# Two transformer blocks on one core: block exchange issued by SyncE, second and third blocks of x by halves

## The chip, the cores and the metric

One Trainium2 chip, one of its cores. The metric is device time in microseconds (us) of one launch that runs both blocks; before the change it is 2243.42 us, the median of three runs (2242.3 to 2247.32). A time is a run of the whole program; a profile is one more execution, with its own time.

## The reference

256 tokens of width 2048 pass through two transformer blocks in float32. The first has a softmax attention with forget gates and a feed-forward part with a causal convolution; the second mixes four gated-linear-attention heads and eight dilated-attention heads, and has a gated feed-forward part.

```python
# first block
a = rms_norm(x, mix_norm)
q, k, v, f = split(a @ fox_w_in)             # 16 heads of 128
q, k = rms_norm(q, q_gain), rms_norm(k, k_gain)
cum = cumsum(log_sigmoid(f + b_f))
p = softmax(causal(q @ k.T * scale + cum_q - cum_k))
h = x + (p @ v) @ fox_w_out
up = rms_norm(h, ffn_norm) @ ffn_w_up        # 2 x 5632 wide
y = conv_b + sum(conv_w[t] * shifted(up, 2 - t) for t in range(3))
gate, val = split(y)
h = h + (silu(gate) * val) @ ffn_w_down
# second block
proj = rms_norm(h, norm1_g) @ w_in_2         # gla q, k, v, r, gate; dilated q, k, v
mix = concat(gla(...) * silu(r), dilated(rms_norm(qb), rms_norm(kb), vb))
h = h + mix @ w_out_2
h2 = rms_norm(h, norm2_g)
out = h + (silu(h2 @ w_gate) * (h2 @ w_up)) @ w_down
```

## The kernel before, in words

Every large product is done by `gemm`. A weight block of 512 rows by 512 columns (1 MB of float32) is loaded into a `raw` tile (`dma_to`, L154; three buffers), split in two halves of a K step each into a rounded part `wh` (ScalarE, ACT, L105) and a rest `wl` (VectorE, DVE, L111), and multiplied as three products, `wh` by the high part of the activations, `wl` by the high part, `wh` by the low part (TensorE, PE, L118 to L120). One unit is such a half: 12 matmuls of 512 columns. `split_to` works four units ahead of the matmuls, with five `wh`/`wl` buffers. The raw buffers come free when the `wl` of their second half is done, so the load of a block waits for DVE.

After each unit `pump` advances the generators in flight by one `yield`: evacuations of finished products (`fast`) and attention (`slow`). So the code's order of emission, unit by unit, sets each engine's order, and each engine and each queue works strictly in that order.

The products leave PSUM with tokens on the partitions; most must be turned so that features are. `flip` (L308) does it without TensorE: DVE transposes 32 by 32 blocks into `turn` (L312), a unit later `exchange` sends `turn` to a DRAM buffer `way` in four DMAs of 128 KB (L303), a unit after that one DMA of 512 KB brings it back with blocks in place (L318), and four units later ACT reads it (`ordered`, L328). Attention's `turned` does the same with the softmax weights (L480, L303, L489). In the kernel before, L303, L318 and L489 are issued by GpSimd's queue (POOL), among POOL's own arithmetic (normalising q and k, L241, L242, L392; the bias tiles `pb`), the loads of forget-gate sums `ckb` (L647, four DMAs of 512 KB that wait for `cum_dram`, L643), and the residual stream's `h` and `home` (L260, L264). SyncE's queue (SP) issues the weights.

`resid` adds the product to `h` (L347). For the first three column blocks it flips `h`; for the last one TensorE transposes it (`transposes`, L290). The `sc` matmuls (L442, L443) read flipped q and k.

At the start `x` comes transposed in four blocks of 512 rows, `xr`; `prep_x` splits a block's four 128-row tiles into high and low (ACT L107, DVE L113). The first block comes by ACT's queue in quarters, the second, third and fourth by SP's (L274), each ahead of its weight block, whose load is in two halves for blocks 1 and 2 (L152). `split_to` prepares a whole block of `x` before the first half of its weight block.

Of the kernel before, what the change touches and what calls it, by code (L numbers as in the profile page):

```python
# [21 lines left out]
KG = D // 512  # L22
# [21 lines left out]
def fox_gla_dilated_kernel(  # L44
# [20 lines left out]
    nc = tc.nc  # L65
# [15 lines left out]
    def alloc(shape, dt, name):  # L81
        i = free_slots.popleft()
        t = slots.tile([P] + shape, dt, tag=f"s{i}", name=name)
        slot_of[id(t)] = (i, t)
        return t

    def free(*ts):
        for t in ts:
            i, _ = slot_of.pop(id(t))
            free_slots.append(i)  # L90
# [9 lines left out]
    def col(c, n=1):  # L100
        return cols[:, c:c + n]

    def hi_of(out_, in_, scale=None):
        if scale is None:
            act.copy(out_, in_)  # L105
        else:
            act.activation(out=out_, in_=in_, func=AF.Copy, scale=scale)  # L107

    def lo_of(out_, in_, hi, scale=None):
        if scale is None:  # L110
            dve.tensor_tensor(out=out_, in0=in_, in1=hi.bitcast(F32), op=ALU.subtract)  # L111
        else:
            dve.scalar_tensor_tensor(  # L113
                out=out_, in0=in_, scalar=scale, in1=hi.bitcast(F32), op0=ALU.mult, op1=ALU.subtract
            )
# [11 lines left out]
    def prep_x(kg, kts=range(4)):  # L127
        for kt in kts:
            d = x_tiles[kg * 2 + kt // 2][:, kt % 2]
            g_ = col(C_MIX + kg * 4 + kt)  # L130
            hi_of(d[:, 0], xr[kg][:, kt], g_)
            lo_of(d[:, 1], xr[kg][:, kt], d[:, 0], g_)
            if kt == 3:
                free(xr[kg])
# [4 lines left out]
    def dma_to(i):  # L139
        while next_dma[0] <= min(i, len(plan) - 1):  # L140
            k = next_dma[0]
            t = rawp.tile([P, 4, 512], F32, tag="raw", name="raw")
            src = plan[k].rearrange("p (k c) -> p k c", c=512)
            if k == 0:
                for q in range(4):
                    nc.sync.dma_start(out=t[:, q], in_=src[:, q])
            else:
                if k < KG:
                    load_x(k)
                if k < 3:  # L150
                    for q in (slice(0, 2), slice(2, 4)):
                        nc.sync.dma_start(out=t[:, q], in_=src[:, q])  # L152
                else:
                    nc.sync.dma_start(out=t, in_=src)  # L154
                if k == 3:
                    nc.sync.dma_start(out=cols[:, C_FFN:], in_=cols_d[:, C_FFN:])
                    nc.sync.dma_start(out=wn, in_=w_n.rearrange("p (a k c) -> p a k c", a=2, c=16))
                if k == 8:
                    nc.sync.dma_start(out=const, in_=const_d)
                if 4 <= k < 8:  # L160
                    fetch(k - 4, nc.sync)
            raw_t[k] = t
            next_dma[0] += 1

    def split_to(u, mid=None):
        while next_spl[0] <= min(u, 2 * len(plan) - 1):
            k = next_spl[0]
            dma_to(k // 2 + NRAW - 1)
            if k in (2, 4, 6):
                prep_x(k // 2)  # L170
            r = raw_t[k // 2][:, (k % 2) * 2:(k % 2) * 2 + 2]
            wh = splp.tile([P, 2, 512], F32R, tag="wh", name="wh")
            wl = splp.tile([P, 2, 512], F32R, tag="wl", name="wl")
            if k < 2:
                for q in range(2):
                    if mid:
                        mid(2 * k + q)
                    hi_of(wh[:, q], r[:, q])
                    lo_of(wl[:, q], r[:, q], wh[:, q])
            else:  # L180
                hi_of(wh, r)
                lo_of(wl, r, wh)
            spl_t[k] = (wh, wl)
            if k % 2:
                raw_t.pop(k // 2)
            next_spl[0] += 1
# [26 lines left out]
    def gemm(xt, kgs, evac, ready=None, last=False):  # L213
        acc = [accp.tile([P, 512], F32, tag="a", name=f"acc{t}") for t in range(2)]
        n = 0
        tot = 4 * len(kgs)
        for kg in kgs:
            while ready is not None and not ready(kg):
                pump()
            for half in range(2):  # L220
                u = unit[0]
                unit[0] += 1
                split_to(u + LEAD)
                wh, wl = spl_t.pop(u)
                xx = xt[kg * 2 + half]
                pairs = [(t, kk) for t in range(2) for kk in range(2)]
                for t, kk in sorted(pairs, key=lambda p: p[1]) if u < 2 else pairs:
                    sl = slice(t * P, (t + 1) * P)
                    mm3(acc[t], xx[:, kk, 0, sl], xx[:, kk, 1, sl], wh[:, kk], wl[:, kk],
                        n + kk == 0, n + kk == tot - 1)  # L230
                n += 2
                if last:
                    free(xx)
                if n == tot:
                    start_fast(evac(acc))
                else:
                    pump()
# [20 lines left out]
    def fetch(c, queue=nc.gpsimd):  # L258
        h[c] = alloc([2, 512], F32, f"h{c}")
        queue.dma_start(out=h[c], in_=home[c])  # L260
# [6 lines left out]
    xr = [alloc([4, S], F32, f"xr{i}") for i in range(KG)]  # L267
    wn = cpool.tile([P, 2, 16, 16], F32, name="wn")
    gqk = cpool.tile([P, 2], F32, name="gqk")

    def load_x(i, kt=None):
        src = x_t[i].rearrange("p (k c) -> p k c", c=S)
        if kt is None:
            nc.sync.dma_start(out=xr[i], in_=src)  # L274
        else:
            nc.scalar.dma_start(out=xr[i][:, kt], in_=src[:, kt])

    rows = {}

# [20 lines left out]
    def exchange(turn, width):  # L300
        way = ways.tile([P, 4, S], F32, tag="way", name="way")
        for i in range(4):
            nc.gpsimd.dma_start(out=way[:, i, 0:width].rearrange("(j c) e -> c j e", c=32),  # L303
                              in_=turn[32 * i:32 * i + 32, :, 0:width])
        return way[:, :, 0:width]

    def flip(src, into=None):
        turn = alloc([4, S], F32, "turn")  # L308
        sv = src.rearrange("p t (k q c) -> p t q k c", q=4, c=32)
        qv = turn.rearrange("p q (k t r) -> p t q k r", t=2, r=32)  # L310
        for t in range(2):
            dve.transpose(out=qv[:, t], in_=sv[:, t])  # L312
        yield
        way = exchange(turn, S)
        yield
        held = alloc([4, S], F32, "flip") if into is None else into
        f = held.rearrange("p a c -> p (a c)").rearrange("p (i e) -> p i e", i=4)
        nc.gpsimd.dma_start(out=f, in_=way)  # L318
        for _ in range(4):
            yield  # L320
        return f.rearrange("p i (k t r) -> p k t i r", k=4, t=2), held, turn
# [93 lines left out]
    def attention(box, gqk, bias_of, ot, done, tag, flipped, ready=None):  # L415
# [58 lines left out]
        def turned(pairs):  # L474
            held = {}
            for a in pairs:
                turn = alloc([4, S], F32, "pturn")
                for n in range(2):
                    pb = sm.pop(a + n)
                    dve.transpose(  # L480
                        out=turn[:, :, n * 96:(n + 1) * 96].rearrange("p j (c r) -> p j c r", c=3),
                        in_=pb[:, 0].rearrange("p (c j r) -> p j c r", c=3, j=4),
                    )
                    free(pb)
                yield
                way = exchange(turn, 192)
                yield
                held[a] = turn
                nc.gpsimd.dma_start(out=turn[:, :, 0:192], in_=way)  # L489
            for _ in range(3):  # L490
                yield
            for a in pairs:
                f = held[a][:, :, 0:192].rearrange("p i (n c r) -> p n c i r", n=2, c=3)
                for n in range(2):
                    pt[a + n] = alloc([3, P], F32, "pts")
                    act.copy(pt[a + n].rearrange("p c (i r) -> p c i r", i=4), f[:, n])
                free(held[a])
                yield
# [28 lines left out]
        if flipped:  # L527
            yield from turned((0, 2))
# [6 lines left out]
    def run_all():  # L535
# [24 lines left out]
        for q in range(1, 4):  # L560
            load_x(0, q)
        pool.memset(mhalf, -0.5)
        act.copy(mhalf[:, 8:16], mhalf[:, 0:8])
        dma_to(0)
        dma_to(2)
        if WARM:
            warm = alloc([2, 512], F32, "warm")
# [7 lines left out]
        xt = x_tiles  # L575

        split_to(1, mid=lambda q: prep_x(0, (q,)))

        def x_rstd():
# [513 lines left out]
```

## Time and profile before

| What | Value |
|---|---|
| median of three runs | 2243.42 us (2242.3 to 2247.32) |
| the profiled execution | 2246.22 us |
| its span, first to last instruction | 2244.4 us |
| PE busy | 2219.1 us (99%), 9888 matmuls |
| DVE busy | 1290.0 us (57%) |
| ACT busy | 1148.9 us (51%) |
| POOL busy | 316.3 us (14%), of it 119.5 us in 216 exchange DMAs of L303 |
| SP's DMA queue (q1), POOL's (q0) | 417.59 MB, 82.39 MB |
| mean granted TensorE clock | 0.997 |

A busy PE is not PE at its peak, since matmuls overlap: the record of one lasts about 390 ns, and they start closer together than that. What a stretch should take is read from the distance between starts. The kernel's end is set by PE, so time is lost where PE waits, or runs at less than its full granted clock.

### The profile page before, as it was taken

Reading aid. Unit: us, or ns where it says so; the run is one execution under the profiler, and the core shown is the slowest. Engines: PE = TensorE matmul, PEld = TensorE weight load, DVE = VectorE, ACT = ScalarE, POOL = GpSimd, SP = SyncE. Lnnn points to the kernel's source line nnn. Section 1 sums busy time; section 2 is a strip of 40 time slices with the busy share of each in tenths; the row PEclk is TensorE's granted clock in tenths of the full one; section 3 lists DMA queues with packets and bytes.
Section 4 is the critical chain, followed back from the end, with each engine's and each line's share of the span. In section 5 each row is a group of like instructions: output and inputs, shape, how many; then the busy total and the mean of one; then the engine's idle time right before and its main releaser. Section 6 shows DMA issues by size and latency. Waiting matters only on the chain.

```text
span 2244.4 us, 25865 instructions
## 1 busy us (share of the span) xinstructions
PE 2219.1 (99%) x9888; PEld 1827.7 (81%) x9888; DVE 1290.0 (57%) x1531; ACT 1148.9 (51%) x1565; POOL 316.3 (14%) x483
## 2 busy tenths in 40 slices
PE   9999999899999999999999999999999999999999
PEld 6788888788888888888887887887888888888887
DVE  5656565466767677654555663555555555554443
ACT  6555555466666656544456654544444444444332
POOL 0453321011111111000222320010000000000000
PEclk9999999999999999999999999999999999999999
DMA  7676657677777777666664773585666666676553
GB/s 297 234 252 209 226 194 245 226 234 252 234 242 243 240 245 245 221 232 236 235 217 168 253 250 135 204 279 193 227 217 212 217 225 214 210 245 228 197 203 116
DMA packets 87403, 502.27 MB, mean 224 GB/s; under 512 B 12560, under 2 KB 14272, under 8 KB 37488
## 3 DMA queue, kind: packets, MB, share of 16 engines
q1 hardware_dynamic: 60272, 417.59, 53.3%
q0 software_dynamic: 26144, 82.39, 11.5%
q8 instruction: 77, 1.26, 0.2%
q10 hardware_dynamic: 864, 0.66, 0.1%
q14 instruction: 46, 0.38, 0.1%
HBM read 459.94 MB, written 40.65 MB: 223 GB/s over the span
## 4 chain that ended last, share of the span: by engine, by line
PE 91%; DMA 4%; ACT 1%; POOL 1%; DVE 1%; issue 1%; ACTq 0%; DVEq 0%; POOLq 0%; SPq 0%
PE acc L118 29%; PE acc L120 29%; PE acc L119 29%; DMA way<-turn 2%; DMA flip<-way 1%; POOL way L303 1%; ACT wh L105 1%; PE sc L443 0%; DMA xr<-in_x_t_dram 0%; DMA way<-pturn 0%; ACT turn L328 0%; PE nar L603 0%; DMA ckb<-cum_dram 0%; DVE h L347 0%; PE sc L442 0%
## 5 line engine op out<-in xcount | busy, mean ns | idle before, releaser
L111 DVE TENSOR_TENSOR wl<-raw,wh 128x1024 fp32r<-128x1024 f32 (+1 forms) x786 | 964.6, 1230 | 816.8 <-ACT wh L105 816.3
L105 ACT CAST wh<-raw 128x1024 fp32r<-128x1024 f32 (+1 forms) x786 | 820.5, 1048 | 793.3 <-PE acc L120 758.7
L118 PE MATMUL acc<-wh,r 128*128 128x512 f32 x1792 | 702.1, 392 | 0.0
L120 PE MATMUL acc<-wh,r 128*128 128x512 f32 x1792 | 698.1, 390 | 0.0
L119 PE MATMUL acc<-wl,r 128*128 128x512 f32 x1792 | 698.0, 390 | 0.0
L118 PEld LDWEIGHTS acc<-wh,r 128*128 128x128 f32 x1792 | 337.1, 188 | 72.0 <-issue 2.5
L120 PEld LDWEIGHTS acc<-wh,r 128*128 128x128 f32 x1792 | 336.8, 188 | 70.5
L119 PEld LDWEIGHTS acc<-wl,r 128*128 128x128 f32 x1792 | 336.9, 188 | 69.3
L118 PE MATMUL acc<-wh,g 128*128 128x512 f32 x704 | 273.9, 389 | 0.0
L119 PE MATMUL acc<-wl,g 128*128 128x512 f32 x704 | 273.9, 389 | 0.0
L120 PE MATMUL acc<-wh,g 128*128 128x512 f32 x704 | 273.9, 389 | 0.0
L303 POOL DMA_DIRECT2D way<-turn x216 | 119.5, 560 | 984.0 <-DVE turn L312 909.0
L118 PE MATMUL acc<-wh,x 128*128 128x512 f32 x384 | 154.5, 402 | 1.2 <-ACT wh L105 1.2
L120 PEld LDWEIGHTS acc<-wh,g 128*128 128x128 f32 x704 | 132.1, 188 | 27.6
L119 PEld LDWEIGHTS acc<-wl,g 128*128 128x128 f32 x704 | 132.1, 188 | 27.5
L118 PEld LDWEIGHTS acc<-wh,g 128*128 128x128 f32 x704 | 132.1, 188 | 27.3
L119 PE MATMUL acc<-wl,x 128*128 128x512 f32 x384 | 149.8, 390 | 0.8 <-DVE wl L111 0.8
L120 PE MATMUL acc<-wh,x 128*128 128x512 f32 x384 | 150.0, 391 | 0.0
L118 PEld LDWEIGHTS acc<-wh,x 128*128 128x128 f32 x384 | 72.4, 189 | 16.6 <-ACT wh L105 1.6
L119 PEld LDWEIGHTS acc<-wl,x 128*128 128x128 f32 x384 | 72.5, 189 | 15.9 <-DVE wl L111 1.3
L120 PEld LDWEIGHTS acc<-wh,x 128*128 128x128 f32 x384 | 72.2, 188 | 15.7
L714 DVE SCALAR_TENSOR_TENSOR u<-turn,cols,u 128x255 f32<-128x255 f32 (+1 forms) x176 | 80.9, 481 | 3.1
(212 smaller groups left out, 1470.0 us busy)
## 6 DMA issues: line engine op xcount, KB each, us to landing
raw<-in_w_dram SPq DMA_DIRECT2D x301, 1024.0 KB, 5.0
raw<-in_w7g_dram SPq DMA_DIRECT2D x44, 1024.0 KB, 4.8
raw<-in_w7u_dram SPq DMA_DIRECT2D x44, 1024.0 KB, 5.0
way<-turn POOLq DMA_DIRECT2D x216, 128.0 KB, 4.7
u<-way POOLq DMA_DIRECT2D x22, 512.0 KB, 5.0
home<-h POOLq DMA_DIRECT2D x12, 512.0 KB, 6.6
h<-home POOLq DMA_DIRECT2D x12, 512.0 KB, 8.4
sg<-way POOLq DMA_DIRECT2D x11, 512.0 KB, 5.6
```

Source lines behind the costliest of these rows:

```text
L105: act.copy(out_, in_)
L111: dve.tensor_tensor(out=out_, in0=in_, in1=hi.bitcast(F32), op=ALU.subtract)
L118: pe.matmul(out_, xh, wh, start=first, stop=False)
L119: pe.matmul(out_, xh, wl, start=False, stop=False)
L120: pe.matmul(out_, xl, wh, start=False, stop=last)
L303: nc.gpsimd.dma_start(out=way[:, i, 0:width].rearrange("(j c) e -> c j e", c=32), in_=turn[32 * i:32 * i + 32, :, 0:width])
L714: dve.scalar_tensor_tensor(out=yy[:, d:S], in0=n[:, kt, 0:S - d], scalar=col(C_CW + 176 - 88 * d + ch), in1=yy[:, d:S], op0=ALU.mult, op1= ...
```

## The change

`exchange` and the DMA that brings the blocks back are issued by `nc.sync` and no longer by `nc.gpsimd`; the units between them and their readers are as they were. For the second and third blocks of `x`, half of the `x` block is loaded ahead of each half of its weight block, all on SP. `prep_x` is called for half a block of `x` ahead of each half of a weight block, for the fourth block of `x` too.

```diff
@@ dma_to
-                if k < KG:
-                    load_x(k)
                 if k < 3:
                     for q in (slice(0, 2), slice(2, 4)):
+                        load_x(k, q, nc.sync)
                         nc.sync.dma_start(out=t[:, q], in_=src[:, q])
                 else:
+                    if k < KG:
+                        load_x(k)
                     nc.sync.dma_start(out=t, in_=src)
@@ split_to
-            if k in (2, 4, 6):
-                prep_x(k // 2)
+            if 2 <= k < 8:
+                prep_x(k // 2, (0, 1) if k % 2 == 0 else (2, 3))
@@ load_x
-    def load_x(i, kt=None):
+    def load_x(i, kt=None, queue=nc.scalar):
-            nc.scalar.dma_start(out=xr[i][:, kt], in_=src[:, kt])
+            queue.dma_start(out=xr[i][:, kt], in_=src[:, kt])
@@ exchange
-            nc.gpsimd.dma_start(out=way[:, i, 0:width].rearrange("(j c) e -> c j e", c=32),
+            nc.sync.dma_start(out=way[:, i, 0:width].rearrange("(j c) e -> c j e", c=32),
@@ flip
-        nc.gpsimd.dma_start(out=f, in_=way)
+        nc.sync.dma_start(out=f, in_=way)
@@ attention, turned
-                nc.gpsimd.dma_start(out=turn[:, :, 0:192], in_=way)
+                nc.sync.dma_start(out=turn[:, :, 0:192], in_=way)
```

POOL's order around the first exchange, that of q and k of the first four heads, in the kernel before:

```order
L392 TENSOR_TENSOR k<-k,rsh 128x1024
L303 DMA way<-turn 32x4x256 x4
L643 DMA cum_dram<-cumts 16x256
L647 DMA ckb_613<-cum_dram 128x1024
...
L647 DMA ckb_619<-cum_dram 128x1024
L318 DMA q<-way 128x1024
L303 DMA way<-turn 32x4x256 x4
L318 DMA k<-way 128x1024
```

The rows of L303 and L318 have left POOL: there `cum_dram` follows `k<-k,rsh` at once. SP's order at the same place, in the kernel after (in the one before SP has `raw` loads alone here):

```order
L304 DMA way<-turn 32x4x256 x4
L155 DMA raw<-in_w_dram 128x2048
L319 DMA q<-way 128x1024
L304 DMA way<-turn 32x4x256 x4
L155 DMA raw<-in_w_dram 128x2048
L319 DMA k<-way 128x1024
L155 DMA raw<-in_w_dram 128x2048 x6
L304 DMA way<-pturn 32x4x192 x4
L490 DMA pturn<-way 128x4x192
```

One weight load stands between a group of `way` and the DMA that brings it back; between `way<-pturn` and `pturn<-way` there is none. In the feed-forward parts the pattern is that of the first three rows, with three or more weight loads behind it.

ACT's order where the second block of `x` is prepared (`xr_84` is that block, `xr_83` the first), in the kernel before:

```order
L107 ACTIVATE x_119<-xr_83,cols 128x256
L105 CAST wh<-raw 128x512
L107 ACTIVATE x_120<-xr_84,cols 128x256 x2
L107 ACTIVATE x_121<-xr_84,cols 128x256 x2
L105 CAST wh<-raw 128x1024 x2
```

Four activations of `x` stand ahead of the two weight casts. The same place in the kernel after:

```order
L107 ACTIVATE x_121<-xr_83,cols 128x256
L105 CAST wh<-raw 128x512
L107 ACTIVATE x_122<-xr_84,cols 128x256 x2
L105 CAST wh<-raw 128x1024
L107 ACTIVATE x_123<-xr_84,cols 128x256 x2
L105 CAST wh<-raw 128x1024
```

Two of the four have moved behind the first weight cast.

## Rows read from the trace of the kernel before

**Rows 1.** Windows: busy us (instructions) by engine, PE clock, DMA share, GB/s.
```profile
9.00:13.00 4.00, 4.00 (x19) 3.19 (x17) 2.13 (x5) 1.74 (x5) 0.00 (x0) 1.00 1.03 410
95.82:98.97 3.15, 3.15 (x8) 2.59 (x9) 2.89 (x4) 3.08 (x5) 3.15 (x4) 0.50 0.92 315
450.00:1100.00 650.00, 650.00 (x2869) 538.22 (x2868) 427.10 (x508) 378.84 (x520) 76.21 (x133) 1.00 0.71 239
```
**Rows 2.** Waits of PE: who waited for whom, total us, times, longest.
```profile
PE tp L290 <- DVE h L347: 12.2, 3, 7.6
PE sc L442 <- ACT turn L328: 5.6, 1, 5.6
...
PE acc L118 <- ACT wh L105: 1.2, 1, 1.2
PE acc L119 <- DVE wl L111: 0.8, 1, 0.8
```
**Rows 3.** Timeline of PE at three waits: start, us, instruction [idle before, releaser].
```profile
89.88 0.39 PE L120 MATMUL acc<-wh,x 128*128 128x512 f32 x1
95.82 0.80 PE L442 MATMUL sc<-turn 128*128 128x128 f32 x2 [5.55 <-ACT turn L328]
...
98.97 0.39 PE L119 MATMUL acc<-wl,x 128*128 128x512 f32 x1
...
400.50 0.39 PE L120 MATMUL acc<-wh,r 128*128 128x512 f32 x1
408.44 2.35 PE L290 MATMUL tp<-const,h 128*128 128x128 f32 x8 [7.55 <-DVE h L347]
...
412.72 0.53 PE L120 MATMUL acc<-wh,r 128*128 128x512 f32 x1
...
1517.39 0.39 PE L120 MATMUL acc<-wh,r 128*128 128x512 f32 x1
...
1525.89 0.40 PE L119 MATMUL acc<-wl,r 128*128 128x512 f32 x1
```
**Rows 4.** Chain that ended last, where the same work did not wait: start, us.
```profile
1129.97 0.87 PE tp L290 x8
...
1210.12 0.43 PE sc L443 x2
```
**Rows 5.** Timeline of POOL around the first exchange.
```profile
74.84 2.15 POOL L647 DMA_DIRECT2D ckb<-cum_dram  x4 [2.45 <-DMA cum_dram<-cumts]
...
91.57 0.56 POOL L318 DMA_DIRECT2D k<-way  x1 [9.43 <-DMA way<-turn]
```
**Rows 6.** Timeline of ACT, the readers of flipped blocks.
```profile
89.77 1.70 ACT L328 ACTIVATE turn<-q,gqk 128x256 f32<-128x256 f32 x4 [12.01 <-DMA q<-way]
...
378.11 1.31 ACT L328 ACTIVATE turn<-flip,cols 128x256 f32<-128x256 f32 x3 [6.06 <-DMA flip<-way]
...
402.84 0.91 ACT L328 ACTIVATE turn<-flip,cols 128x256 f32<-128x256 f32 x2 [5.24 <-DMA flip<-way]
...
1516.55 0.91 ACT L328 ACTIVATE turn<-flip,cols 128x256 f32<-128x256 f32 x2 [5.85 <-DMA flip<-way]
```
**Rows 7.** Timeline of DVE, two block transposes that an exchange sends.
```profile
70.51 1.29 DVE L312 STREAM_TRANSPOSE turn<-k 128x512 f32<-128x512 f32 x2
...
385.32 1.30 DVE L312 STREAM_TRANSPOSE turn<-h 128x512 f32<-128x512 f32 x2
```
**Rows 8.** DMA issues: count, KB each, median us from issue to landing.
```profile
raw<-in_w_dram SPq DMA_DIRECT2D x301, 1024.0 KB, 5.0
...
way<-turn POOLq DMA_DIRECT2D x216, 128.0 KB, 4.7
```
**Rows 9.** Timeline of ACT, second block of x.
```profile
11.77 1.71 ACT L107 ACTIVATE x<-xr,cols 128x256 fp32r<-128x256 f32 x4 [2.26 <-DMA xr<-in_x_t_dram]
```
**Rows 10.** Waits: of SP's queue, and of all engines.
```profile
SPq L154 <- DVE wl L111: 1925.6, 371, 17.0
...
ACT wh L105 <- DMA raw<-in_w_dram: 9.9, 4, 5.5
```

## The prediction

> **What bounds the kernel now.** I read the windows first. From 450 to 1100 us TensorE (PE) is busy for 650 us of 650, at a granted clock of 1.00, with 2869 matmuls: 226.6 ns from one start to the next [rows 1]. The first feed-forward part therefore runs at PE's own pace, and nothing done to a queue makes it faster. Then I read PE's waits: there are few. Three times in all it waits for `h` before the `tp` transposes (12.2 us), once for the flipped block that `sc` reads (5.6 us), and at the start once for a weight cast and once for its rest (1.2 and 0.8 us) [rows 2]. All that a change can give back lies there and in what follows there.
>
> The timeline shows what follows. Each of the three long waits costs more than its idle time, since the matmuls behind it are slow for a while: the stretch 95.82 to 98.97 us has a granted clock of 0.50, which is 1.2 GHz of 2.4, after PE had stood idle for 5.55 us [rows 1, 3]. So I take the loss from starts, not from idle time. Units are 226.6 ns for a matmul of a product, 0.87 us for the eight `tp` and 0.43 us for a pair of `sc`, of which there are two, taken alike [rows 1, 4].
>
> - First wait: from the start at 89.88 to the start at 98.97 are 9.09 us [rows 3]. In it lie five product matmuls (the one at 89.88 and four behind `sc`, 1.13 us) and two pairs of `sc` (0.86 us), together 1.99. Lost: 7.1 us.
> - Second: 400.50 to 412.72, 12.22 us [rows 3], with six product matmuls (1.36 us) and `tp` (0.87), 2.23. Lost: 10.0 us.
> - Third: 1517.39 to 1525.89, 8.50 us [rows 3], with five product matmuls and `tp`, 2.00. Lost: 6.5 us.
>
> Together 23.6 us. All three lead to the exchange by POOL's queue. In the first, ACT stood for 12.01 us at 89.77 until the block of q had come back, and POOL could send the block of k back only at 91.57, after 9.43 us of waiting for `way`, with four `ckb` loads of 512 KB (from 74.84 us) ahead in its queue [rows 5, 6]. In the second and third, ACT stood for 5.24 and 5.85 us on a flipped block [rows 6]; the casts behind it, DVE's rest of them and DVE's addition to `h` came late by as much, and PE, in order, stood at `tp`.
>
> **The change part by part.** *The exchange on SP's queue.* What does an exchange take there? The trace has none on SP, so I bound it. A weight load of 1024 KB on SP lands 5.0 us after its issue, a `way` of 128 KB on POOL after 4.7 [rows 8]. A leg of an exchange moves 512 KB. Above: four issues at POOL's pace of 0.54 us (2.15 us for four DMAs) [rows 5], then 5.0 us for each of two legs, 12.2 us. Below: 7.2 us, if a leg with half the bytes of a weight load takes half its 5.0. I take 9, between them, since a weight load may stand between the two legs.
>
> First wait: the block of k is turned by 71.80 us (70.51 + 1.29) [rows 7]. With 12.2 us it is back at 84.0; if all of the `ckb` transfer, 2 MB, which at 410 GB/s is 5.1 us [rows 1], stood in its way too, at 89.1. PE would want `sc` at 90.1 (89.88 + 0.23). So this wait goes even by the upper bound, though with 1 us to spare; by 9 us, with 4 to 9. If the cover fails the cost is what it is now, 7.1 us, at most.
>
> Second: turned at 386.62 (385.32 + 1.30) [rows 7], back by POOL when ACT began at 402.84 [rows 6], so 16.2 us; ACT wanted it 5.24 earlier, after 11.0 us. With 9 us it is early by 2; with 12.2 late by 1.2, but the turn itself will be earlier, since ACT had stood 6.06 us at 378.11 on the exchange before it [rows 6], which goes too. The third is the same stage of the second block; ACT wanted the block 5.85 us earlier, and I have no bound that differs. So all 23.6 us go, with nothing else late at these places: the `tp` at 1129.97, where the exchange was long done, took its 0.87 us without a wait [rows 4].
>
> What SP now does late: every weight load behind the four `way` (which wait for DVE's turn) and behind the DMA that brings them back (which waits for `way`). Who waits for that is ACT's weight cast, then DVE, then PE four units later. The cover is SP's idle time: it waited 1925.6 us in 371 loads for a raw buffer, 5.2 us for each load [rows 10], and a leg takes at most 5.0 us. ACT waited for a weight load only 9.9 us in all, four times [rows 10]. I cost this at nothing; without the cover it is the third rival. POOL loses 216 issues of L303 and those of the way back; PE does not wait for POOL's arithmetic, so that is worth nothing. The `home` and `h` transfers leave POOL earlier, since the way back no longer stands ahead, and share the DMA engines with the exchange: that is inside the 12.2.
>
> *The halves of x.* In 9 to 13 us the DMA engines are full, 410 GB/s [rows 1]. With halves, 256 KB less lie ahead of the first half of `x` and of the first half of the weights: 262144 bytes at 410 GB/s, 0.64 us. ACT, which began at 11.77 with four activations in 1.71 us [rows 9], does two of them (0.86 us) ahead of the cast. So the cast can come earlier by 0.64 us, if it only follows the bytes, up to 1.5 us (0.64 + 0.86), if it only follows ACT. Bounds: nothing (the bytes' order gives no gain) and 2.0 us (all of the two waits) [rows 2]. I take 1.0. The second halves land when they did; their cast has a unit of matmuls, 2.7 us, to hide in.
>
> Sum: 23.6 + 1.0 = 24.6 us from the profiled execution's 2246.2 (1.8 us more than its span) gives 2221.6. That execution was 2.8 us above the median of the runs, so for a median I forecast 2243.4 - 24.6 = 2218.8, rounded to 2219.
>
> The rule that speaks against it: the Trainium skill, "DMA: Bandwidth & Descriptors", section "Issuing engines are not separate DMA queues", says that DMAs of all issuing engines run on the same 16 DMA engines, and that issuing from several saves only the time of the issue. By it the transfers would be as slow from SP as from POOL, and the sum 1.0 us, not 24.6. No run here shows an exchange from SP; that a block of q waited behind `ckb` in one queue [rows 5, 6] does not agree with it.
>
> The same page, section "Queues, rings and completion order", says that a DMA engine takes turns between the queues that have work. By it an exchange on SP's queue stands behind the weight load issued before it and no longer takes turns with it; at 410 GB/s a whole weight load ahead is 2.6 us as an estimate, which the 12.2 us above hold.
>
> **The rivals.**
>
> *One of the three waits stays.* The first is the likeliest: `ckb` still crosses the exchange, and the margin by the upper bound is 1 us. The second has the `home` and `h` transfers beside it. Against: the 9 us leave some us at both. Price 6.5 to 10.0 us back: 2225 to 2229.
>
> *The exchange is no faster on SP.* The transfer and not the queue sets it: then only the start gains, 2243.4 - 1.0 = 2242. For it: `way` was waited for 9.43 us where its median landing is 4.7 [rows 5, 8], so something beside the queue may delay it. Against: POOL's order names what delays it in the first place.
>
> *SP is blocked and the weights come late.* Place: attention, where `pturn<-way` stands right behind `way<-pturn` in SP's order and nothing can issue while `way` lands; there are ten such pairs (two for each of the five groups of heads that are flipped). Price: if `way` takes the 9.43 us that POOL saw, each pair blocks SP for 4.2 us more than the 5.2 us that a load's wait covers; if PE felt all of it, ten cost 42 us: 2219 + 42 = 2261. It decides from a block of 5.2 us on, and only when what ACT and DVE have split ahead is used up, four units of 2.7 us, which is why I hold it unlikely.
>
> **How the numbers follow.** Forecast 0.68; one wait stays 0.17; no faster on SP 0.09; SP blocked 0.06. A change of 0.2%, 4.5 us, is what a measurement here can tell from none. The forecast and the first rival are both faster by more: 0.85. The second rival is within it: 0.09. The third is slower: 0.06. Range: below, all of the 2.0 us at the start and 1.5 us of spread between medians, 2216; above, the largest wait stays, 2229, with 2 us of spread, 2231. What lies outside is the last two rivals, 0.15.
>
> **What would show it.** PE's waits for `tp` and `sc` are gone from the list, and with them the stretches at half the clock. ACT's idle time before L328 is near zero, and SP's idle time for DVE is smaller by what the exchange takes. At the start PE's wait for the first cast of the second block is 1 us shorter. The forecast is wrong if ACT still waits for flipped blocks at the two places where `h` is turned, if ACT's waits for weight loads grow past some 20 us, or if new waits of PE appear in attention.

## The result, and the profile after

The kernel after takes 2220.1 us in the median (2219.57 to 2220.35, four runs), the kernel before on the same chip 2245.1 (2242.3 to 2247.32, four runs). The ratio is 0.9889, with a 95% interval of 0.9872 to 0.9906: 25.0 us saved, where 24.6 were forecast. Medians of before went from 2243 to 2248 us between comparisons, so kernels of different comparisons are set side by side by their ratios.

The profiled execution's span is 2218.5 us, 25.9 less than before. PE's waits come first. Columns: who waited for whom, us in total, times, longest.

```profile
PE warm L572 <- DVE warm L569: 1.4, 1, 1.4
PE acc L119 <- DVE wl L111: 0.7, 1, 0.7
```

This is the whole list. The three waits for `tp` and the one for `sc` [rows 2] are gone; the first line is PE's warm-up ahead of all work. The same three windows as in [rows 1], in the kernel after:

```profile
9.00:13.00 4.00, 4.00 (x19) 3.29 (x19) 2.42 (x5) 2.49 (x5) 0.00 (x0) 1.00 1.03 409
95.82:98.97 3.15, 3.15 (x16) 2.62 (x15) 2.33 (x7) 1.65 (x6) 0.00 (x0) 1.00 0.76 307
450.00:1100.00 650.00, 650.00 (x2870) 538.60 (x2869) 424.01 (x498) 374.81 (x510) 14.78 (x18) 1.00 0.70 238
```

The second window has 16 matmuls at a granted clock of 1.00, where it had 8 at 0.50. The third has 2870 matmuls for 2869: at PE's own pace, as before. PE's timeline at the two places that answer to the first two stretches of [rows 3]:

```profile
88.79 0.38 PE L443 MATMUL sc<-turn 128*128 128x128 f32 x2
89.00 0.60 PE L444 MATMUL sc<-turn 128*128 128x256 f32 x2
89.25 0.58 PE L118 MATMUL acc<-wh,x 128*128 128x512 f32 x1
...
391.63 1.03 PE L291 MATMUL tp<-const,h 128*128 128x128 f32 x8
392.42 0.47 PE L118 MATMUL acc<-wh,r 128*128 128x512 f32 x1
```

No idle time stands behind a row: `sc` starts when PE comes to it, and `tp` too. Where the 25.9 us came from is read by setting the start of each product matmul of one trace against the same one of the other. By that the start of the program gave 1.6 us (matmul 0 to matmul 25), the first wait 7.3, the second 10.1, the third 6.5, and a place near 280 us, in attention, another 0.4: 25.9.

Then the exchange. SP's queue at the first one, that of q and k:

```profile
65.34 1.78 SPq L304 DMA_DIRECT2D way<-turn  x4
67.22 0.39 SPq L155 DMA_DIRECT2D raw<-in_w_dram  x1
69.92 0.34 SPq L319 DMA_DIRECT2D q<-way  x1
70.50 2.01 SPq L304 DMA_DIRECT2D way<-turn  x4
72.56 0.49 SPq L155 DMA_DIRECT2D raw<-in_w_dram  x1
76.44 0.34 SPq L319 DMA_DIRECT2D k<-way  x1
```

The way back of k is issued at 76.44 us, where POOL came to it at 91.57 [rows 5]. ACT's timeline: the second block of `x`, then readers of flipped blocks.

```profile
10.75 0.91 ACT L107 ACTIVATE x<-xr,cols 128x256 fp32r<-128x256 f32 x2 [0.94 <-DMA xr<-in_x_t_dram]
12.05 1.05 ACT L105 CAST wh<-raw 128x1024 fp32r<-128x1024 f32 x1 [0.40 <-DMA raw<-in_w_dram]
...
76.34 1.71 ACT L329 ACTIVATE turn<-q,gqk 128x256 f32<-128x256 f32 x4
...
84.50 1.34 ACT L329 ACTIVATE turn<-k 128x256 f32<-128x256 f32 x4
...
384.63 1.70 ACT L329 ACTIVATE turn<-flip,cols 128x256 f32<-128x256 f32 x4
```

The readers that stood for 12.01 and 5.24 us [rows 6] stand for nothing. The price on SP, in waits (SP's queue, then ACT), and the landing of a weight load, of a `way`, and of a `way` of attention's softmax weights (KB each, median us from issue to landing):

```profile
SPq L155 <- DVE wl L111: 1408.5, 313, 11.5
SPq L304 <- DVE turn L313: 181.0, 50, 5.2
SPq L319 <- DMA way<-turn: 105.4, 98, 3.5
SPq L490 <- DMA way<-pturn: 29.9, 23, 5.0
...
ACT wh L105 <- DMA raw<-in_w_dram: 9.4, 9, 2.8
```
```profile
raw<-in_w_dram SPq DMA_DIRECT2D x301, 1024.0 KB, 5.2
...
way<-turn SPq DMA_DIRECT2D x216, 128.0 KB, 2.7
...
way<-pturn SPq DMA_DIRECT2D x40, 96.0 KB, 5.4
```

SP's idle time for DVE fell from 1925.6 us [rows 10] to 1408.5, and ACT waits for weight loads as little as before (9.4 us for 9.9). A `way` lands in 2.7 us where POOL's took 4.7 [rows 8]; one of the softmax weights takes 5.4, where POOL's took 4.6.

### The profile page after: what moved, and what is told of

The parts are those of the page before. It is cut to its first block, busy times and chain, and to the rows that moved or that the text cites. A ratio compares the mean times of both kernels' runs of the same rounds, so it can differ in the third digit from the quotient of the medians.

```text
span 2218.5 us, 25858 instructions
## 1 busy us (share of the span) xinstructions
PE 2212.7 (100%) x9888; PEld 1825.2 (82%) x9888; DVE 1291.4 (58%) x1531; ACT 1154.2 (52%) x1565; POOL 135.5 (6%) x163
## 4 chain that ended last, share of the span: by engine, by line
PE 99%; DMA 0%; DVE 0%; ACT 0%; SPq 0%; DVEq 0%; issue 0%
PE acc L118 32%; PE acc L120 32%; PE acc L119 32%; PE sc L444 0%; PE nar L604 0%; DMA raw<-in_w_dram 0%; PE cs L870 0%; PE sc L443 0%; PE ov L508 0%; PE ov L507 0%; PE ov L506 0%; PE tp L291 0%; DMA xr<-in_x_t_dram 0%; PE o L900 0%; PE o L895 0%; PE narow L614 0%
## 5 line engine op out<-in xcount | busy, mean ns | idle before, releaser
L119 PEld LDWEIGHTS acc<-wl,g 128*128 128x128 f32 x704 | 132.2, 188 | 27.3
L118 PEld LDWEIGHTS acc<-wh,g 128*128 128x128 f32 x704 | 132.2, 188 | 27.3
L120 PEld LDWEIGHTS acc<-wh,x 128*128 128x128 f32 x384 | 72.1, 188 | 15.4
L261 POOL DMA_DIRECT2D h<-home x12 | 6.7, 555 | 918.0 <-issue 455.1
```

Of the source, the lines that this page charges most:

```text
L118: pe.matmul(out_, xh, wh, start=first, stop=False)
L119: pe.matmul(out_, xh, wl, start=False, stop=False)
L120: pe.matmul(out_, xl, wh, start=False, stop=last)
```

## Experiments

The theory after the comparison: an exchange on SP is short enough for its readers, and that alone gives the three waits back. Its rivals: one part of POOL's load (`ckb`) or one of the two legs does it all, or the readers' place does.

**One part of the change alone.** First the exchange on SP with `x` in whole blocks:

```diff
+                if k < KG:
+                    load_x(k)
                 if k < 3:
                     for q in (slice(0, 2), slice(2, 4)):
-                        load_x(k, q, nc.sync)
                         nc.sync.dma_start(out=t[:, q], in_=src[:, q])
...
-            if 2 <= k < 8:
-                prep_x(k // 2, (0, 1) if k % 2 == 0 else (2, 3))
+            if k in (2, 4, 6):
+                prep_x(k // 2)
```

> Exchange on SP, blocks of x whole as before. Theory (the three waits of PE come from the exchange's place in POOL's queue, the start from the order of the halves): 23.9 of the 25.5 us stay, so 2221.7 us, 1.6 above the changed kernel's 2220.1; PE's waits for tp and sc gone, the two of the start (1.2 and 0.8 us) back. Rival (the halves matter for more than the start, because everything behind them comes earlier): 2225 us or more.

Measured: 2221.9 us (2220.68 to 2223.3), ratio 0.9888 [0.9875, 0.9900]; span 2221.1. Waits of PE at the start, and a window behind them:

```profile
PE acc L118 <- ACT wh L105: 1.0, 1, 1.0
PE acc L119 <- DVE wl L111: 0.9, 2, 0.8
```
```profile
15.00:19.00 4.00, 3.75 (x10) 2.97 (x11) 4.00 (x7) 3.69 (x6) 0.00 (x0) 0.59 1.04 428
```

The exchange alone gives nearly everything. The spans of the two profiles differ by 2.6 us, more than the waits of 1.9: here PE's clock was at 0.59 in the mean of 15 to 19 us, so part of the window ran at the lower level. The kernel before, with waits of 1.2 and 0.8 us at the same place, had 1.00 in that window, and its start was 1.5 us shorter by starts of matmuls; so this part is not what whole blocks of `x` cost. The ratios of the two kernels can't be told apart.

Then the halves, with all of the exchange on POOL:

```diff
-            nc.sync.dma_start(out=way[:, i, 0:width].rearrange("(j c) e -> c j e", c=32),
+            nc.gpsimd.dma_start(out=way[:, i, 0:width].rearrange("(j c) e -> c j e", c=32),
...
-        nc.sync.dma_start(out=f, in_=way)
+        nc.gpsimd.dma_start(out=f, in_=way)
...
-                nc.sync.dma_start(out=turn[:, :, 0:192], in_=way)
+                nc.gpsimd.dma_start(out=turn[:, :, 0:192], in_=way)
```

> Halves of x, exchange on POOL. Theory: before less 1.6 us, about 2243.5, the three waits of PE (5.6 for sc, 12.2 for tp) as before. Rival: the halves move the first exchange away from the ckb loads, the wait for sc shrinks by over 3 us and the time is 2240 or less.

Measured: 2243.2 us (2237.98 to 2248.03), ratio 0.9981 [0.9971, 0.9991].

```profile
PE tp L291 <- DVE h L348: 10.1, 2, 5.2
PE sc L443 <- ACT turn L329: 5.8, 1, 5.8
```

The waits of before are there. The gain at the start, by starts of matmuls, is 1.8 us; the ratio says 2 to 6.5, which also holds the spread of the long waits from run to run.

Then, with the halves, the nine flips of `h` on SP and all else on POOL:

```diff
-        way = exchange(turn, S)
+        way = exchange(turn, S, queue)
...
-        nc.gpsimd.dma_start(out=f, in_=way)
+        queue.dma_start(out=f, in_=way)
...
-                f, held, turn = yield from flip(h[cb])
+                f, held, turn = yield from flip(h[cb], queue=nc.sync)
```

> Changed kernel, but only the nine flips of the residual stream h go by SP, all others by POOL. Theory (each wait is made by the exchange of its own stage): the second and third waits (10.0 and 6.4 us) stay gone, the first (7.3 us) and 0.5 us near 285 us come back: 2220.1 + 7.8 = 2227.9. Rival (SP helps because POOL's queue as a whole is emptied, and the load of it matters everywhere): nearer to 2240.

Measured: 2228.3 us (2227.75 to 2230.51), ratio 0.9918 [0.9905, 0.9930]. One long wait of PE is left:

```profile
PE sc L443 <- ACT turn L329: 4.8, 1, 4.8
```

So the second and third waits belong to the exchanges of `h` and the first to those of q and k, as their places said.

**What makes the first exchange late.** `ckb` taken out of POOL's queue, the exchange left there (and the halves):

```diff
-            pool.dma_start(out=sc, in_=cs[0:16])
+            nc.sync.dma_start(out=sc, in_=cs[0:16])
-                pool.dma_start(out=ckb[g], in_=sc[g * 4:(g + 1) * 4, :].unsqueeze(0).to_broadcast([P, 4, S]))
+                nc.sync.dma_start(out=ckb[g], in_=sc[g * 4:(g + 1) * 4, :].unsqueeze(0).to_broadcast([P, 4, S]))
```

> Halves of x, exchange on POOL, but the forget-gate sums (cum_dram and the four ckb loads of 512 KB) go by SP. Theory (the first wait is the blocks of q and k standing behind ckb in one queue): the wait for sc is gone, the two for tp stay: 2243.5 - 7.3 = 2236. Rival (it is the load on the DMA engines, 2 MB of ckb, whatever queue issues it): the wait for sc stays near 5.6 us, 2243 or more.

Measured: 2246.5 us (2243.94 to 2248.55), ratio 0.9996 [0.9987, 1.0005]. The theory fell: nothing was gained. POOL's timeline there:

```profile
67.86 2.42 POOL L304 DMA_DIRECT2D way<-turn  x4
77.41 0.57 POOL L319 DMA_DIRECT2D q<-way  x1 [7.13 <-DMA way<-turn]
77.97 2.19 POOL L304 DMA_DIRECT2D way<-turn  x4
89.51 0.56 POOL L319 DMA_DIRECT2D k<-way  x1 [9.36 <-DMA way<-turn]
```

No `ckb` stands in this queue, and `way` is still waited for 7.13 and 9.36 us: its 512 KB share the DMA engines with `ckb` and weight loads that SP has already issued. So I took bytes away too: with the exchange on POOL, only the first `ckb` stays, and the others follow six units apart.

```diff
             for g in range(4):
+                for _ in range(6 if g else 0):
+                    yield
                 ckb[g] = alloc([4, S], F32, f"ckb{g}")
...
-                                  lambda: ckb[3] is not None))
+                                  lambda g=g: ckb[g] is not None))
```

> The halves of x with the exchange on POOL, as in the run with the halves alone (2243.2 us), and of the four ckb loads only the first near the first exchange; the other three follow six units apart, so 1.5 MB less cross it. Theory C (the bytes of ckb on shared engines and in POOL's order were what made the first exchange late): the sc wait of 5.6 us is gone, PE's first loss of 7.1 us with it, and the two tp waits (10 us) stay: 2236 us. Theory A (POOL's legs take turns with weight loads whatever ckb does): the sc wait shrinks by what 1.5 MB take at 410 GB/s, 3.8 us, and no more: 1 to 3 us of wait are left, 2239 to 2241 us. Rival (ckb has no part in it, as the run with ckb on SP might suggest): 2243 us.

Measured: 2240.9 us (2232.95 to 2247.55), ratio 0.9972 [0.9959, 0.9984]. The readers of q and k on ACT:

```profile
81.29 1.71 ACT L329 ACTIVATE turn<-q,gqk 128x256 f32<-128x256 f32 x4 [5.10 <-DMA q<-way]
...
92.49 1.33 ACT L329 ACTIVATE turn<-k 128x256 f32<-128x256 f32 x4 [5.51 <-DMA k<-way]
```

In the kernel with the halves alone ACT had come to q at 87.79 us and to k at 93.37. q is back 6.5 us earlier now, k 0.9, and PE's wait for `sc` only went from 5.8 to 4.3 us. Theory C, bytes of `ckb` alone, fell; of theory A the direction held, and the wait left over was larger than its 1 to 3 us.

**One leg alone.** `way` on POOL and the way back on SP, from the kernel after:

```diff
-            nc.sync.dma_start(out=way[:, i, 0:width].rearrange("(j c) e -> c j e", c=32),
+            nc.gpsimd.dma_start(out=way[:, i, 0:width].rearrange("(j c) e -> c j e", c=32),
```

> The kernel after, with only the four DMAs that send a block out (way) issued by POOL again; the one that brings it back stays on SP. Theory A (on POOL's queue a leg takes turns with weight loads already queued on SP, so it lands late while the DMA engines are full; on SP's queue it stands ahead of the loads issued after it): way lands at 4.5 us or more in the median as before, against 2.7 after, and SP, waiting for it, holds back the weight loads. PE waits for tp or sc again, less than before (12.2 and 5.6 us), and the time is 2225 to 2232 us. Theory B (only POOL's order, ckb ahead of the way back, made the exchange late): way has no one ahead of it on POOL, so the time is that of the kernel after, 2220 us within 2, with no wait of PE for tp or sc. Third (the prediction's rival, SP blocked by a slow way): weight loads come late and ACT's waits for raw go from 9 to over 20 us, with new waits of PE in attention: above 2245 us.

Measured: 2225.6 us (2224.83 to 2226.62), ratio 0.9908 [0.9893, 0.9923]. POOL sends k, then ACT reads it:

```profile
72.81 2.14 POOL L648 DMA_DIRECT2D ckb<-cum_dram  x4 [2.49 <-DMA cum_dram<-cumts]
74.95 2.22 POOL L304 DMA_DIRECT2D way<-turn  x4
```
```profile
91.12 1.33 ACT L329 ACTIVATE turn<-k 128x256 f32<-128x256 f32 x4 [7.26 <-DMA k<-way]
```

k is sent behind `ckb`, 4.5 us later than by SP (70.50), and PE waits 3.4 us at `sc`. There is no `tp` wait. Theory A's time (2225 to 2232) held, and its `way` too, which lands in 4.8 us here; theory B's 2220 fell. Weight loads came late more often, as the third rival has it (ACT waited 27.3 us for them, not 9.4), and PE did not feel it.

The other leg: `way` on SP, the way back on POOL.

```diff
-        nc.sync.dma_start(out=f, in_=way)
+        nc.gpsimd.dma_start(out=f, in_=way)
-                nc.sync.dma_start(out=turn[:, :, 0:192], in_=way)
+                nc.gpsimd.dma_start(out=turn[:, :, 0:192], in_=way)
```

> The kernel after, with only the DMA that brings a block back (q, k, h, pturn, u <- way) issued by POOL; way stays on SP. Theory A (each leg on POOL takes turns with weight loads): way lands at 2.7 us as after, the way back at 6 to 9 us where the engines are full. One leg of two is late, so half of what before lost comes back at most: no tp waits or under 3 us of them, at the first exchange, where ckb stands ahead on POOL, an sc wait of 2 to 5 us: 2222 to 2230 us. Theory B (only POOL's order): the first exchange loses all of its 7 us, since k<-way stands behind ckb, and the tp waits are gone: 2227 us. Rival (no leg matters by itself): 2220 us within 2.

Measured: 2228.9 us (2227.99 to 2229.4), ratio 0.9922 [0.9907, 0.9937].

```profile
73.20 2.15 POOL L648 DMA_DIRECT2D ckb<-cum_dram  x4 [5.15 <-DMA cum_dram<-cumts]
75.34 0.54 POOL L319 DMA_DIRECT2D q<-way  x1
```
```profile
88.50 1.70 ACT L329 ACTIVATE turn<-q,gqk 128x256 f32<-128x256 f32 x4 [12.86 <-DMA q<-way]
```

Theory B has it to 2 us (theory A's 2222 to 2230 holds it as well, but its wait for `sc` was to be 5 us at most, and is 6.4): the first exchange loses its 7 us, because q's way back stands behind four `ckb`, and the waits for `tp` are gone. So each leg on POOL is late at the first exchange for a reason of its own, and only both on SP make it early.

**The readers' place.** The kernel after with the readers one unit, and in a second kernel three (`range(3)`), after the way back, and not four:

```diff
-        for _ in range(4):
+        for _ in range(1):
             yield
```

> The kernel after, with the readers of a flipped block one unit after the way back and not four: 8.2 us earlier in ACT's order. This takes away the slack that the kept readers give. From turn to return the exchange takes about 11 us beside full DMA engines (first exchange, block of q: 65.3 us to 75.1 us) and readers now come after about 3 units, 8.2 us. Theory (the exchange is short enough that slack, not its length, covers it): ACT waits 1 to 4 us for each flipped block, 5 x 9 or more of them, but the casts run four units ahead, so PE waits nowhere in the feed-forward parts; at h's flips the tp comes no earlier, since it is set by the last block, and waits stay below 2 us: 2220 us within 3. Rival (each wait of ACT reaches PE by DVE as in before): waits of tp and sc come back, 2228 us or more.

Measured: 2338.9 us (2337.61 to 2340.78), ratio 1.0415 [1.0397, 1.0432].

```profile
ACT turn L329 <- DMA u<-way: 191.9, 22, 10.2
ACT turn L329 <- DMA flip<-way: 65.8, 9, 9.2
...
PE acc L118 <- ACT wh L105: 25.8, 18, 2.7
```

My expectation was far off: I held that the casts' lead of four units would cover ACT, and it was used up at nearly every exchange. PE's waits add up to 71 us, and its mean granted clock fell to 0.986. The cover has an end, and it had not been seen: in the kernel after 53 of 54 exchanges are back before their readers' turn, and in the kernel before an exchange is late by 0.5 us in the median.

> The kernel after, with the readers three units after the way back and not four. An exchange has from the issue of way to the readers five units of 2.72 us, 13.6 us, in the kernels before and after; here four, 10.9 us. In the trace of after, an exchange takes 9.7 us in the median from the first way's issue to the landing of the way back; 11 of 54 take longer than 10.9 us, by 12.5 us in all; one takes over 13.6. Theory S (the exchange's length against this slot decides, the queue only sets the length): small waits of ACT for flipped blocks, 10 to 40 us in all; PE feels at most half of the 12.5 us: 2221 to 2227 us. Rival (readers' order against the casts matters by itself, as the 118 us lost with one unit might also say): a third of that loss, about 2260 us.

Measured: 2219.9 us (2219.03 to 2220.61), ratio 0.9881 [0.9866, 0.9896], level with the kernel after. ACT waits a little for flipped blocks, PE not at all:

```profile
ACT turn L329 <- DMA u<-way: 26.7, 20, 4.1
...
ACT turn L329 <- DMA flip<-way: 10.8, 7, 3.1
```

That made a rule to test from the other side. From the issue of `way` to its readers the code gives an exchange five units of 2.72 us, 13.6 us: its slot. POOL's exchange should then do as well as SP's with a longer one. On the kernel with the halves alone, readers five units and, in a second kernel, six (`range(6)`) after the way back:

```diff
-        for _ in range(4):
+        for _ in range(0, 5):
             yield
```

> The exchange left on POOL's queue as before, with the halves of x (2243.2 us), and the readers five units after the way back and not four: 16.3 us for an exchange and not 13.6. In the trace of the run with the halves alone an exchange takes 14.1 us in the median; 39 of 54 are over 13.6 us, by 44.5 us in all, and 4 over 16.3, by 6.7 us in all, the block of q (20.5) and of k (17.7) of the first exchange among them, and one before the first tp wait (17.2). Theory S (length against slot): the tp waits go from 10.1 to under 2 us, the sc wait from 5.8 to 2 to 4 us: 2223 to 2229 us, with the queue as slow as it was. Rival (the queue itself costs, by POOL's arithmetic or the shared DMA engines, or the later readers make the next stage late): 2240 us or more.

Measured: 2232.5 us (2229.22 to 2235.8), ratio 0.9937 [0.9919, 0.9956].

```profile
PE sc L443 <- ACT turn L329: 5.8, 1, 5.8
PE ov L506 <- ACT pts L497: 5.1, 1, 5.1
```

> As the run before it, with the readers six units after the way back: 19.0 us for an exchange. One exchange of 54 is longer than that, the block of q of the first, by 1.5 us. Theory S (length against slot): no tp wait, the sc wait under 2 us: 2220 to 2223 us, level with the exchange on SP's queue. Rival (queue itself, or readers so late that attention's end and the last transposes of a residual come late): 2230 us or more, with new waits of PE.

Measured: 2238.4 us (2235.9 to 2241.74), ratio 0.9965 [0.9951, 0.9980].

```profile
PE ov L506 <- ACT pts L497: 7.5, 5, 3.3
```

Half of the rule held: with POOL's queue as slow as it was, both `tp` waits went. The first exchange did not, since it took 23.3 us here and not 20.5, and a new wait came in attention, where the flipped softmax weights are late for `ov`. So a longer slot is no substitute for the shorter exchange in this kernel. Why attention's exchanges came late behind later readers was not tried.

The lengths, from the traces: first issue of `way` to the landing of the way back, us.

| Kernel | slot | median of 54 | nine flips of h | first q, k | PE waits tp; sc |
|---|---|---|---|---|---|
| before | 13.6 | 14.1 | 12.1 to 17.6 | 20.2, 17.7 | 12.2; 5.6 |
| `ckb` spread, POOL | 13.6 | 14.1 | 12.1 to 17.9 | 13.3, 17.9 | 11.9; 4.3 |
| `way` POOL, back SP | 13.6 | 12.0 | 11.8 to 13.6 | 8.4, 16.1 | 0; 3.4 |
| `way` SP, back POOL | 13.6 | 9.7 | 9.1 to 11.0 | 23.9, 20.0 | 0; 6.4 |
| after | 13.6 | 9.6 | 10.6 to 12.4 | 9.7, 13.7 | 0; 0 |
| after, three units | 10.9 | 9.9 | 10.6 to 14.1 | 10.2, 14.1 | 0; 0 |
| after, one unit | 5.4 | 10.0 | 10.6 to 12.4 | 9.7, 13.5 | 3.0; 21.5 |
| POOL, five units | 16.3 | 14.1 | 12.3 to 16.8 | 23.3, 20.6 | 0; 5.8 |
| POOL, six units | 19.0 | 14.3 | 12.1 to 15.4 | 21.6, 21.3 | 0; 3.9 |

An overrun did not cost by itself: in the kernel before 43 of 54 exchanges were longer than their slot, with readers after three units 13, and in the latter PE waited for none. What the table doesn't show is which flips of `h` are followed by a wait. In two of the three stages that add to `h` the three flips come 22 to 27 us apart, and there, with POOL's exchange and readers after four units, PE's wait at `tp` was the sum of the three overruns:

| Kernel | overruns added up; wait, first such stage | the same, second |
|---|---|---|
| before | 7.4; 7.6 | 4.3; 4.6 |
| halves alone | 4.9; 5.0 | 5.1; 5.2 |
| `ckb` on SP | 7.1; 7.2 | 4.2; 4.4 |
| `ckb` spread | 5.3; 5.8 | 6.0; 6.1 |

In the third stage, where the flips are some 60 us apart, sums of 1.9 to 3.3 us in these kernels cost nothing, and with readers after three units 2.0 and 3.4 us in the two stages cost nothing either. Why the overruns add up was not tried. With one unit all 54 overrun, by 4.7 us in the mean.

**The rest at the start.** In the kernel after, the first half of the second block of `x` and of its weights by quarters, with PE's order in that unit to match:

```diff
-                    for q in (slice(0, 2), slice(2, 4)):
+                    for q in ((0, 1, slice(2, 4)) if k == 1 else (slice(0, 2), slice(2, 4))):
...
-            if 2 <= k < 8:
+            if 3 <= k < 8:
...
-            if k < 2:
+            if k < 3:
...
-                    if mid:
+                    if k == 2:
+                        prep_x(1, (q,))
+                    if mid and k < 2:
...
-                for t, kk in sorted(pairs, key=lambda p: p[1]) if u < 2 else pairs:
+                for t, kk in sorted(pairs, key=lambda p: p[1]) if u < 3 else pairs:
```

> The kernel after, with the first half of the second block of x and of its weights loaded and split by quarters. PE's waits in the kernel after are 1.4 us at its first instructions and 0.7 us for the first wl of the second block; nothing else is left. Theory (the bytes that stand ahead set the second): it goes to 0.3 us or less, and the time is 0.5 to 0.8 us less than that of the kernel after, 2219.5 us, which is hardly to be told from it. Rival (each DMA issued on SP takes 0.4 to 0.5 us, so two more issues eat what the smaller pieces save): the wait stays at 0.7 us or grows to 1.5 us, 2220 to 2221 us.

Measured: 2220.3 us (2219.71 to 2220.43), ratio 0.9882 [0.9868, 0.9897].

```profile
PE acc L119 <- DVE wl L111: 0.2, 1, 0.2
```

The wait shrank as the theory had it, from 0.7 to 0.2 us, and the time can't be told from that of the kernel after. No version here is faster than the kernel after by more than the noise.

## Why the prediction came out right, and where it was off

*PE's waits and their cost by starts.* Right: 7.1, 10.0 and 6.5 us forecast, 7.3, 10.1 and 6.5 found. Idle time alone would have given 17.8 [rows 2]. The kernel with only the flips of `h` on SP and the two with one part of the change each put the terms at their places.

*The exchange takes 9 us on SP, 7.2 to 12.2.* 9.6 in the median of the 54. The gain is in the first leg: from the first issue to the landing of all four `way` it went from 8.1 to 4.4 us, between the legs from 0.6 to 0.1, and the second leg from 5.2 to 5.0 (medians); with the way back alone on POOL the whole is 9.7 us too. The ten exchanges of attention went another way: 7.0 to 6.6 us in the first leg, 5.1 to 3.7 in the second. The upper bound did not hold for four of the 54. The longest is k of the first exchange, 13.7 us, which shares the engines with `ckb`; it landed at 84.2 us, where the sum with that bound had 84.0, because the exchange began earlier.

*The mechanism of the first wait was part of it only.* The prediction named `ckb` ahead in POOL's queue. With it out of that queue the 7 us stayed; with three quarters of its bytes out of the way 1.6 us of them went. What is shown is that for this wait both legs must leave POOL's queue; for the second and third, one leg on SP was enough, whichever it was. The forecast of the first came out because the change took both legs away at once, and not because `ckb` ahead was the whole cause.

That sharing with loads already issued on SP is the rest of it fits the 7 to 9 us waits for `way` without `ckb` ahead, and the traces bear it out. With `way` on POOL and the way back on SP, 19 `way<-pturn` by POOL had no transfer in flight beside them but the exchange's own, and landed in 2.2 to 2.5 us; nine that had one for over three quarters of their time took 3.9 to 7.2. In the kernel before 84 of 216 `way<-turn` had another transfer beside them all along and took 6.3 us in the median, where 35 with one for less than three quarters of their time took 2.4; in the kernel after those with one all along are 40. So POOL's queue is not slow by itself. This compares transfers within a trace: no run took the weight loads away. Nor did a run issue the exchange from ACT's queue, which would tell leaving POOL's queue from standing in SP's.

The Trainium skill, "DMA: Bandwidth & Descriptors", section "Queues, rings and completion order", has a DMA engine take turns between queues; the late `way` beside weight loads in the run with `ckb` on SP agrees with it (7.13 and 9.36 us). The Trainium skill's section "Issuing engines are not separate DMA queues" on that page grants another engine only the time of the issue. The measurement differs: four issues take 1.78 us on SP for 2.19 on POOL (medians), 0.4 us, while the first leg is 3.7 us shorter; by that rule the time would have stayed near 2242, and it is 2220.

*SP's waits cost nothing.* Right. SP waited 105.4 us for `way` at L319 and 29.9 us for it at L490, at most 5.0 us at once, under the 5.2 us from which the third rival would decide. The larger part is another: 181.0 us at L304 for DVE's turn, 50 times, at most 5.2 us, which just meets that limit. With `way` on POOL ACT's waits for weights tripled, and PE still did not feel it.

*The start, 1.0 us: the term that was too small.* 1.6 us by starts. The half of `x` landed about 1.0 us earlier than the whole block had and the half of the weights as well (0.64 was reckoned from bytes); ACT's order gave the rest. The bounds, nothing to 2.0, held it.

*One wait stays.* It came nearest at the first exchange: k was read at 84.50 us, without a wait, 0.3 us after it had landed.

## What to carry to other kernels

Measure the length of a round trip through a queue and set it against the time that the code's order leaves for it. Below that it cost nothing here. Above it the cost depended on what came behind: nothing where the next exchange was far, and all of the overruns together, with the slow clock behind them, where three came 22 to 27 us apart. An exchange that someone waits for can go by the queue that carries the prefetches, ahead of those that have slack, if the queue's own idle time covers one leg, as it did here; taking one neighbour out of the slow queue helps less than it seems, and its readers can't be put off without moving what comes after them.

## What was not expected of the hardware

The same transfers go in more packets by SP's queue than by POOL's, and the flipped blocks' `way` still lands sooner. The page's line on packets, of before and then of after:

```profile
DMA packets 87403, 502.27 MB, mean 224 GB/s; under 512 B 12560, under 2 KB 14272, under 8 KB 37488
```
```profile
DMA packets 116429, 502.28 MB, mean 226 GB/s; under 512 B 12593, under 2 KB 51393, under 8 KB 66513
```

With the bytes the same, 37,121 more packets are under 2 KB, and a `way<-turn` lands in 2.7 us for 4.7. In attention it is the other way round: a `way<-pturn` lands in 5.4 us for 4.6.

What the exchange gained at its first use, `ckb` paid. POOL in the kernel after:

```profile
73.89 2.15 POOL L648 DMA_DIRECT2D ckb<-cum_dram  x4 [5.04 <-DMA cum_dram<-cumts]
82.92 1.03 POOL L657 TENSOR_SCALAR pb<-ckb,cum 128x128 f32<-128x128 f32 x1 [6.89 <-DMA ckb<-cum_dram]
```

The first of the four landed 8.9 us after its issue and the last 18.0 us after (6.5 and 11.9 in the kernel before), each of 512 KB, with SP's transfers beside them; the bias tiles that need them were still in time.
